# Two passes of 512 and 256 columns for three of 256: both parts of the activations side by side under one weight tile

## The chip, the cores and the metric

The kernel runs on one core of one Trainium2 chip. The metric is the device time of one execution in microseconds. TensorE (PE) multiplies, VectorE (DVE), ScalarE (ACT) and GpSimd (POOL) do the rest, and SyncE (SP) issues most of the transfers.

## The reference

Two networks of two layers each run one behind the other on 256 tokens of 1024 features, batch 1, in float32. The first network (conditioning, neighbourhood attention beside a matrix memory, a delta-rule recurrence, squared-ReLU MLPs) also carries 256 context tokens through its first layer. The second has swiglu stages around two mixers and a memory attention. The parts that the change reaches, cut to the products:

```python
def _swiglu(h, w_gu, w_down):                      # w_gu 1024 x 5632, w_down 2816 x 1024
    gate, up = jnp.split(h @ w_gu, 2, axis=-1)
    return (jax.nn.silu(gate) * up) @ w_down

def squared_relu_mlp(h, w1, w2):                   # w1 1024 x 4096, w2 4096 x 1024
    return jnp.square(jax.nn.relu(h @ w1)) @ w2

# first network, layer 1, after its recurrence
x = x + gt_a * o_l                                 # o_l = (...) @ w_o, 1024 x 1024
x = x + gt_m * squared_relu_mlp(modulate(x, sh_m, sc_m), mlp_w1[1], mlp_w2[1])
# second network
for layer in range(2):
    x = x + 0.5 * _swiglu(_rmsnorm(x, ffn_pre_norm[layer]), ...)
    x = x + (_even_mixer if layer == 0 else _mla_mixer)(_rmsnorm(x, mix_norm[layer]), ...)
    x = x + _memory_cross_attention(_rmsnorm(x, xmem_norm[layer]), ...)
    x = x + 0.5 * _swiglu(_rmsnorm(x, ffn_post_norm[layer]), ...)
```

## The kernel before

Activations lie with features on partitions: `x` is eight tiles of 128 features by 256 tokens. Each operand of a product is split into two float32r parts, a high one (`wh`, `xh`) and a low one (`wl`, `xl`), whose sum is exact. `mm3` then takes three passes: high by high, high by low, low by high. Each pass is one matmul with its own load of the stationary operand, a weight unit of 128 by 128.

Weights come as a `Stream` of units. Its `load` fetches a tile of 2048 columns, 1 MB, from SP's queue into one of two `raw` buffers. Each half of 1024 columns, eight units, is copied to `wh` on ScalarE (L71) and the remainder put into `wl` on VectorE (L72); there are four buffers of each, so splits run up to four halves ahead of the products.

`gemm_a` computes a product with features on partitions: for each feature tile of the result it takes a bank `g` of PSUM and runs `mm3` over the feature tiles of the input, with the stationary weight unit and 256 columns (the tokens) moving; then `evac` evicts the bank. In layer 0's MLP the moving operand has 512 columns, since tokens and context tokens stand side by side (`n_cols`). `gemm_b` has the activations stationary and is not touched.

The users of `gemm_a` with 256 columns all lie in the second half of the program: the recurrence's output product (`rwkv_out`, `wo`, with the first three tiles in two cuts), `mlp` with one stream (`mlp1`, `mlp2`), the four swiglu stages (`ffn`; gate and up run the same loop by hand, a gate and an up tile in one bank), `u`, `q` and `k` of the even mixer, and three output projections (`proj_out`). Units: 64, 256 and 256, 4 x (352 + 176), 96, 192.

A stage begins with a norm. `pre_norm` scales each feature tile (`xg`, VectorE), copies the high part (ScalarE, L167), subtracts for the low part (VectorE, L168), and squares it (ScalarE) for a sum that POOL gathers (L495); two matmuls into `t` (L248) add over the partitions. A swiglu applies 1/rms only at its eviction. The order on each engine is set by a scheduler from the order of the code and the tiles' dependencies; each engine then runs its list in order.

Of the kernel before, what the change touches and what calls it, by code (L numbers as in the profile page):

```python
# [9 lines left out]
F32 = mybir.dt.float32  # L10
# [8 lines left out]
P = 128  # L19
# [10 lines left out]
class Stream:  # L30
    """A weight matrix as a row of [128, nb] units, loaded in tiles of WCOL
    columns and split into two float32r parts whose sum is exact."""
# [11 lines left out]
    def load(self, t):  # L44
        """a tile of the matrix on its way"""
# [34 lines left out]
class KB:  # L80
# [32 lines left out]
    def open_psum(self, **banks):  # L113
        """all of PSUM: banks per pool"""
# [4 lines left out]
    def open_gemm(self, n=4):  # L119
        """the pools of the products with weights"""  # L120
# [21 lines left out]
    def row_in(self, name, n, pool=None):  # L142
        """a row of n numbers, the same in all partitions"""
# [8 lines left out]
    def act_set(self, after, name):  # L152
        """load a named activation table right behind an instruction"""
# [5 lines left out]
    def mm3(self, ps, wh, wl, xh, xl, start, stop):  # L159
        """ps += (wh + wl).T @ (xh + xl) in three float32r passes"""  # L160
# [3 lines left out]
        mm(ps, wl, xh, start=False, stop=stop)  # L164

# [55 lines left out]
    def rstd_tok(self, sums, n, width, scale, eps):  # L221
        """(sums * scale + eps) ** -0.5 on a [128, n] tile"""
# [7 lines left out]
    def sumsq(self, pool, xs, kt):  # L230
        """for each x the sum over its feature tiles of x squared: [128, T], the partitions still to add"""
# [12 lines left out]
    def rstd_from(self, acc, n_feat):  # L244
        """token-major 1/rms [128, 2] from the squares' partial sums"""
# [5 lines left out]
    def bcast_tok(self, rs, pool, col=0, n=2):  # L251
        """rs [128 tokens, n] -> [128, n * 128], the same row in all partitions"""
# [11 lines left out]
class Phase:  # L264
    """pools of one phase: tag -> number of buffers, opened together"""
# [20 lines left out]
def bc(ap, axis, n):  # L286
    """ap with a new axis of n equal entries at free position axis"""
# [2853 lines left out]
```

## Time and profile before

| | us |
|---|---|
| median of 3 runs | 2860.93 |
| lowest, highest | 2856.49, 2864.15 |
| profiled execution, span from the first to the last instruction | 2854.8 |
| PE busy in it | 2654.0 (93%) |
| VectorE busy | 1763.1 (62%) |
| ScalarE busy | 1297.4 (45%) |

For the profiled execution the page gives the span only; what lies around it is not in the page. Busy times are unions, so overlapping products count once. The profile's groups bear the line of the helper that issued an instruction, which is why all products stand under L162 to L164 and are told apart by their tiles' names: `xnh`, `xnl` are a normed input's parts, `hh`, `hl` a swiglu's inner activations or an MLP's input, `dh`, `dl` an MLP's inner activations, `ch`, `cl` the input of an output projection.

### The profile page before, as it was taken

What the parts mean: (1) busy time and instruction counts of PE and PEld (TensorE: products, weight loads), DVE (VectorE), ACT (ScalarE), POOL (GpSimd) and SP (SyncE); (2) the same over time, 40 slices, a digit from 0 to 9 for tenths busy, and PEclk for the clock granted to TensorE, in tenths of its full rate; (3) what the DMA queues carried; (4) which work ended last, traced back from release to release, by engine and by line L of the source; (5) the groups of instructions that cost most, each with busy time, mean ns of one, the idle gap of its engine ahead of it and who ended that gap; (6) DMA issues with size and microseconds to landing.
All of it is one profiled execution on the core that took longest, in us unless ns stands there. A gap on an engine that the chain in (4) does not pass through costs nothing.

```text
span 2854.8 us, 52905 instructions
## 1 busy us (share of the span) xinstructions
PE 2654.0 (93%) x22052; PEld 2362.1 (83%) x22052; DVE 1763.1 (62%) x2885; ACT 1297.4 (45%) x2358; POOL 402.5 (14%) x392
## 2 busy tenths in 40 slices
PE   5999999999968879887899999999999999799999
PEld 3977567888757666765899999998999999798999
DVE  4453564334386966885774665776665665765764
ACT  3344333223245541675553544555444444655443
POOL 1210100000044552342100001011001001311100
PEclk9999989999978889998999999999999999999999
DMA  7244735223223675323455455433455554233554
GB/s 274 89 156 152 260 126 191 103 89 104 83 72 107 226 228 114 81 68 96 139 186 179 170 183 198 163 134 119 167 188 177 178 186 172 96 105 110 177 178 148
DMA packets 108142, 426.29 MB, mean 149 GB/s; under 512 B 14334, under 2 KB 50430, under 8 KB 66046
## 3 DMA queue, kind: packets, MB, share of 16 engines
q1 hardware_dynamic: 107326, 420.76, 43.1%
q8 instruction: 173, 2.83, 0.4%
q10 hardware_dynamic: 576, 2.15, 0.2%
q14 instruction: 67, 0.55, 0.1%
HBM read 397.68 MB, written 24.13 MB: 148 GB/s over the span
## 4 chain that ended last, share of the span: by engine, by line
PE 78%; DVE 13%; ACT 4%; POOL 2%; issue 2%; DMA 1%; SPq 0%; ACTq 0%; DVEq 0%; POOLq 0%
PE g L162 20%; PE g L163 20%; PE g L164 20%; PE pG L162 2%; PE pG L163 2%; PE pG L164 2%; DVE pr L2605 2%; DVE N L2607 2%; PE d L1343 2%; PE pX L2623 1%; DVE wl L72 1%; PE pA L2551 1%; POOL acc L495 1%; DVE we L2558 1%; POOL rs L227 1%
## 5 line engine op out<-in xcount | busy, mean ns | idle before, releaser
L72 DVE TENSOR_TENSOR wl<-raw,wh 128x1024 fp32r<-128x1024 f32 x512 | 626.9, 1225 | 427.7 <-ACT wh L71 425.5
L71 ACT CAST wh<-raw 128x1024 fp32r<-128x1024 f32 x512 | 535.2, 1047 | 638.0 <-PE g L163 546.2
L163 PE MATMUL g<-xnl,wh 128*128 128x256 f32 x1504 | 427.9, 285 | 1.0 <-DVE xnl L168 1.0
L162 PE MATMUL g<-xnh,wh 128*128 128x256 f32 x1504 | 427.4, 285 | 1.3 <-ACT xnh L167 1.3
L164 PE MATMUL g<-xnh,wl 128*128 128x256 f32 x1504 | 427.9, 285 | 0.0
L162 PE MATMUL g<-hh,wh 128*128 128x256 f32 (+1 forms) x1216 | 374.4, 308 | 4.9 <-ACT wh L71 3.4
L164 PE MATMUL g<-hh,wl 128*128 128x256 f32 (+1 forms) x1216 | 373.3, 307 | 0.7 <-DVE wl L72 0.7
L163 PE MATMUL g<-hl,wh 128*128 128x256 f32 (+1 forms) x1216 | 373.9, 308 | 0.0
L162 PEld LDWEIGHTS g<-xnh,wh 128*128 128x128 f32 x1504 | 290.5, 193 | 1.7 <-ACT xnh L167 1.7
L163 PEld LDWEIGHTS g<-xnl,wh 128*128 128x128 f32 x1504 | 290.6, 193 | 1.5 <-DVE xnl L168 1.5
L164 PEld LDWEIGHTS g<-xnh,wl 128*128 128x128 f32 x1504 | 290.7, 193 | 0.0
L162 PEld LDWEIGHTS g<-hh,wh 128*128 128x128 f32 x1216 | 234.6, 193 | 17.5 <-ACT wh L71 4.0
L163 PEld LDWEIGHTS g<-hl,wh 128*128 128x128 f32 x1216 | 234.3, 193 | 14.2 <-DVE hl L1382 2.5
L164 PEld LDWEIGHTS g<-hh,wl 128*128 128x128 f32 x1216 | 234.1, 193 | 12.5 <-issue 1.7
L495 POOL TENSOR_TENSOR acc<-acc,sq 128x256 f32<-128x256 f32 x63 | 65.8, 1045 | 863.5 <-ACT sq L494 381.2
L162 PE MATMUL g<-dh,wh 128*128 128x512 f32 (+1 forms) x512 | 172.0, 336 | 0.0
L163 PE MATMUL g<-dl,wh 128*128 128x512 f32 (+1 forms) x512 | 172.0, 336 | 0.0
L164 PE MATMUL g<-dh,wl 128*128 128x512 f32 (+1 forms) x512 | 172.0, 336 | 0.0
L2623 PE MATMUL pX<-ident 128*128 128x256 f32 (+3 forms) x388 | 106.9, 386 | 32.8 <-DVE N L2607 17.9
L163 PE MATMUL g<-wl,hh 128*128 128x256 f32 x448 | 128.4, 287 | 6.9 <-DVE wl L72 6.9
L162 PE MATMUL g<-wh,hh 128*128 128x256 f32 x448 | 131.2, 293 | 3.3 <-ACT wh L71 3.2
L164 PE MATMUL g<-wh,hl 128*128 128x256 f32 x448 | 127.8, 285 | 0.0
(590 smaller groups left out, 5961.7 us busy)
## 6 DMA issues: line engine op xcount, KB each, us to landing
raw<-in_w_mlp SPq DMA_DIRECT2D x64, 1024.0 KB, 4.8
raw<-in_w_ada SPq DMA_DIRECT2D x48, 1024.0 KB, 6.3
raw<-in_w_pre_gu SPq DMA_DIRECT2D x44, 1024.0 KB, 4.8
raw<-in_w_post_gu SPq DMA_DIRECT2D x44, 1024.0 KB, 4.8
raw<-in_w_pre_down SPq DMA_DIRECT2D x22, 1024.0 KB, 4.8
raw<-in_w_post_down SPq DMA_DIRECT2D x22, 1024.0 KB, 4.8
raw<-in_w_ab SPq DMA_DIRECT2D x14, 1024.0 KB, 4.9
d_bk<-h SPq DMA_DIRECT2D x16, 512.0 KB, 3.0
```

What stands on the lines that cost most here:

```text
L71: nc.scalar.copy(h[:, :w], r)
L72: nc.vector.tensor_tensor(l[:, :w], r, h[:, :w].bitcast(F32), op=ALU.subtract)
L162: mm(ps, wh, xh, start=start, stop=False)
L163: mm(ps, wh, xl, start=False, stop=False)
L164: mm(ps, wl, xh, start=False, stop=stop)
L227: nc.gpsimd.tensor_tensor(rs[:, :n], ms[:, :n], self.mhalf[:, :n], op=ALU.pow)
L495: nc.gpsimd.tensor_tensor(acc, acc, sq, op=ALU.add)
L1343: nc.tensor.matmul(ps[32 * j : 32 * j + 32], self.cpad[:, k0 + j, 30 - 2 * n : 62 - 2 * n], raw[:, j * 512 : (j + 1) * 512], start=n == 0 ...
L2551: nc.tensor.matmul(ps[64:, i], bk[:64, i0 + i], we[0][:64, :W, i0 + i], start=True, stop=True)
L2605: nc.vector.tensor_tensor(pr, bc(N[:, k + 1 :, k], 2, k), bc(N[:, k, :k], 1, m), op=ALU.mult)
L2607: row = nc.vector.tensor_tensor(N[:, k + 1 :, :k], N[:, k + 1 :, :k], pr, op=ALU.add)
L2623: mm = self.nc.tensor.matmul(o, self.ident, bc(self.ident[:, :64], 1, cols // 64), start=True, stop=True)
```

## The change

The two parts of an activation become the two halves of one tile: `x2[:, k]` holds 256 columns of the high part and then 256 of the low one. `mm2` multiplies the high weights with all 512 columns in one pass, into a whole bank, and the low weights with the high half in a second pass, into the bank's first half. The bank's two halves must still be added, so each eviction reads both: `both` copies one half on ScalarE and adds the other on VectorE, and an eviction that adds to `x` does so twice. `gemm_w` is `gemm_a` with `mm2`. Gate and up of a swiglu can no longer share a bank; up goes to a bank of the pool `psa`. In the MLP the ReLU moves from ScalarE's eviction into VectorE's square. The core of the diff:

```diff
+    def mm2(self, ps, wh, wl, x, start, stop):
+        mm = self.nc.tensor.matmul
+        mm(ps, wh, x, start=start, stop=False)
+        mm(ps[:, 0], wl, x[:, 0], start=False, stop=stop)
+
+    def halves(self, ps):
+        return ps.rearrange("p (a t) -> p a t", a=2)
+
+    def both(self, out, ps):
+        self.nc.scalar.copy(out, ps[:, 1])
+        self.nc.vector.tensor_tensor(out, ps[:, 0], out, op=ALU.add)
+
+    def gemm_w(self, st, nt, kt, x, evac, lead=0, cuts=2):
...
+        for n in range(lead, nt):
+            o = self.halves(self.psg.tile([P, 512], F32, name="g"))
+            for k in range(kt):
+                wh, wl = st.next()
+                self.mm2(o, wh, wl, x(k), k == 0, k == kt - 1)
+            evac(n, o)
...
     def pre_norm(self, ph, gain, x=None, tagx="xn"):
...
-        xh = ph.tile(tagx + "h", [P, KT, T], F32R)
-        xl = ph.tile(tagx + "l", [P, KT, T], F32R)
+        self.x2 = ph.tile(tagx + "h", [P, KT, 2, T], F32R)
+        xh, xl = self.x2[:, :, 0], self.x2[:, :, 1]
...
     def ffn(self, which, l):
...
-                ps = self.psg.tile([P, 512], F32, name="g").rearrange("p (z t) -> p z t", z=2)
-                for z in range(2):
+                gu = ph.tile("gu", [P, 2, T])
+                for z, (pool, name) in enumerate(((self.psg, "g"), (self.psa, "a"))):
+                    ps = self.halves(pool.tile([P, 512], F32, name=name))
                     for k in range(KT):
                         wh, wl = st.next()
-                        self.mm3(ps[:, z], wh, wl, xh[:, k], xl[:, k], k == 0, k == KT - 1)
-                gu = ph.tile("gu", [P, 2, T])
-                nc.vector.tensor_tensor(gu, ps, bc(rb, 1, 2), op=ALU.mult)
+                        self.mm2(ps, wh, wl, x2[:, k], k == 0, k == KT - 1)
+                    self.both(gu[:, z], ps)
+                nc.vector.tensor_tensor(gu, gu, bc(rb, 1, 2), op=ALU.mult)
...
             def evac(n, ps):
-                nc.vector.scalar_tensor_tensor(self.x[:, n], ps, 0.5, self.x[:, n], op0=ALU.mult, op1=ALU.add)
-
-            self.gemm_a(st, KT, FT, lambda k: hh[:, k], lambda k: hl[:, k], evac)
+                for a in range(2):
+                    nc.vector.scalar_tensor_tensor(self.x[:, n], ps[:, a], 0.5, self.x[:, n], op0=ALU.mult, op1=ALU.add)
+
+            self.gemm_w(st, KT, FT, lambda k: h2[:, k], evac)
...
     def mlp(self, l, mods, ns, between=None):
...
-                    nc.scalar.activation(r, ps, AF.Relu)
-                    nc.vector.tensor_tensor(r, r, r, op=ALU.mult)
+                    if ns == 1:
+                        self.both(r, ps)
+                        nc.vector.scalar_tensor_tensor(r, r, 0.0, r, op0=ALU.max, op1=ALU.mult)
```

The other evictions (`proj_out`, `rwkv_out`, `mlp2`, `u`, `q`, `k`) change in the same two ways. The transfers, POOL's list and everything before the recurrence's output product keep their order.

Three places show what moves on the engines. On PE, in a gate and up stage of the first swiglu, before (`g_...` is the bank, the numbers name one buffer):

```order
L162 MATMUL g_15801<-xnh_14538,wh_15832 128x256
L163 MATMUL g_15801<-xnl_14539,wh_15832 128x256
L164 MATMUL g_15801<-xnh_14538,wl_15833 128x256
L162 MATMUL g_15801<-xnh_14538,wh_15832 128x256
L163 MATMUL g_15801<-xnl_14539,wh_15832 128x256
L164 MATMUL g_15801<-xnh_14538,wl_15833 128x256
```

and with the change:

```order
L170 MATMUL g_14955<-xnh_14001,wh_14958 128x512
L171 MATMUL g_14955<-xnh_14001,wl_14959 128x256
L170 MATMUL g_14955<-xnh_14001,wh_14958 128x512
L171 MATMUL g_14955<-xnh_14001,wl_14959 128x256
L170 MATMUL a_14980<-xnh_14001,wh_14981 128x512
L171 MATMUL a_14980<-xnh_14001,wl_14982 128x256
```

Three products of 256 columns for a weight unit became one of 512 and one of 256; up's units go to a bank `a`.

On VectorE in the same stage, before (`wl` is a split of weights, `gu` the multiplication with 1/rms, `gs` the product of the two halves, `hl` the low part of the result):

```order
L72 TENSOR_TENSOR wl_15767<-raw_15736,wh_15766 128x1024
L522 TENSOR_TENSOR gs_15664<-gs_15664,gu_15662 128x256
L168 TENSOR_TENSOR hl_14612<-gs_15664,hh_14611 128x256
L72 TENSOR_TENSOR wl_15805<-raw_15802,wh_15804 128x1024
L519 TENSOR_TENSOR gu_15728<-g_15669,rb_14609 128x512
L72 TENSOR_TENSOR wl_15833<-raw_15802,wh_15832 128x1024
L522 TENSOR_TENSOR gs_15730<-gs_15730,gu_15728 128x256
```

and with the change (L179 is the addition in `both`, L552 the multiplication with 1/rms, L555 the product, L200 the low part):

```order
L179 TENSOR_TENSOR gu_14844<-g_14845,gu_14844 128x256
L72 TENSOR_TENSOR wl_14982<-raw_14956,wh_14981 128x1024
L179 TENSOR_TENSOR gu_14844<-a_14870,gu_14844 128x256
L552 TENSOR_TENSOR gu_14844<-gu_14844,rb_14071 128x512
L72 TENSOR_TENSOR wl_15014<-raw_15011,wh_15013 128x1024
L555 TENSOR_TENSOR gs_14894<-gs_14894,gu_14844 128x256
L179 TENSOR_TENSOR gu_14899<-g_14900,gu_14899 128x256
L200 TENSOR_TENSOR hh_14073<-gs_14894,hh_14073 128x256
L179 TENSOR_TENSOR gu_14899<-a_14925,gu_14899 128x256
```

Two additions per pair of tiles stand between the splits of weights; the multiplication now reads their result.

On VectorE at the end of `mlp2` and the entry of the first swiglu, before (L1880 evicts the last bank, L486 scales, L168 takes the low part):

```order
L1880 SCALAR_TENSOR_TENSOR x_11285<-g_14383,mods1_103,x_11285 128x256
L486 TENSOR_SCALAR xg_14540<-x_11285,k_vecs2_73 128x256
L486 TENSOR_SCALAR xg_14544<-x_11285,k_vecs2_73 128x256
L72 TENSOR_TENSOR wl_14711<-raw_14680,wh_14710 128x1024
L168 TENSOR_TENSOR xnl_14539<-xg_14540,xnh_14538 128x256
L168 TENSOR_TENSOR xnl_14539<-xg_14544,xnh_14538 128x256
```

and with the change (L1931 evicts, L518 scales, L200 takes the low part):

```order
L1931 SCALAR_TENSOR_TENSOR x_11285<-g_13883,mods1_103,x_11285 128x256
L518 TENSOR_SCALAR xg_14002<-x_11285,k_vecs2_73 128x256
L1931 SCALAR_TENSOR_TENSOR x_11285<-g_13883,mods1_103,x_11285 128x256
L518 TENSOR_SCALAR xg_14006<-x_11285,k_vecs2_73 128x256
L200 TENSOR_TENSOR xnh_14001<-xg_14002,xnh_14001 128x256
L72 TENSOR_TENSOR wl_14157<-raw_14131,wh_14156 128x1024
L200 TENSOR_TENSOR xnh_14001<-xg_14006,xnh_14001 128x256
```

A second evicting pass stands behind the first scaling, and a split of weights moved behind the first low part.

## Rows read from the trace of the kernel before

**Rows 1.** the page, the chain that ended last: shares of the span, by engine and by line

```profile
PE 78%; DVE 13%; ACT 4%; POOL 2%; issue 2%; DMA 1%; SPq 0%; ACTq 0%; DVEq 0%; POOLq 0%
PE g L162 20%; PE g L163 20%; PE g L164 20%; PE pG L162 2%; PE pG L163 2%; PE pG L164 2%; DVE pr L2605 2%; DVE N L2607 2%; PE d L1343 2%; PE pX L2623 1%; DVE wl L72 1%; PE pA L2551 1%; POOL acc L495 1%; DVE we L2558 1%; POOL rs L227 1%
```

**Rows 2.** stretches; busy us (with instructions) of PE, PEld, DVE, ACT, POOL; granted clock, DMA, GB/s

```profile
1388.10:1396.80 8.70, 7.83 (x33) 7.24 (x34) 7.05 (x13) 4.93 (x8) 0.00 (x0) 0.50 0.25 75
1485.00:1577.20 92.20, 92.20 (x770) 92.17 (x769) 47.96 (x56) 36.80 (x43) 0.00 (x0) 1.00 0.55 187
1577.20:1589.10 11.90, 8.78 (x52) 7.73 (x51) 10.37 (x21) 6.92 (x18) 6.61 (x8) 0.86 0.31 110
1589.10:1710.80 121.70, 121.70 (x1017) 121.70 (x1016) 82.81 (x106) 59.66 (x87) 0.00 (x0) 1.00 0.53 180
```

**Rows 3.** the timeline of PE in a gate and up stage: start, modelled duration, product

```profile
1649.94 0.28 PE L162 MATMUL g<-xnh,wh 128*128 128x256 f32 x1
...
1651.14 0.28 PE L163 MATMUL g<-xnl,wh 128*128 128x256 f32 x1
```

**Rows 4.** the timeline of PE in layer 0's squared-ReLU MLP

```profile
640.04 0.39 PE L162 MATMUL g<-hh,wh 128*128 128x512 f32 x1
...
641.40 0.39 PE L162 MATMUL g<-hh,wh 128*128 128x512 f32 x1
```

**Rows 5.** groups of products by line and shape: count, busy us, mean ns of one

```profile
L162 PE MATMUL g<-xnh,wh 128*128 128x256 f32 x1504 | 427.4, 285 | 1.3 <-ACT xnh L167 1.3
L162 PE MATMUL g<-hh,wh 128*128 128x256 f32 x960 | 273.5, 285 | 3.4 <-ACT wh L71 3.4
...
L162 PE MATMUL g<-ch,wh 128*128 128x256 f32 x256 | 73.1, 288 | 1.4 <-ACT ch L167 1.4
...
L162 PE MATMUL g<-dh,wh 128*128 128x256 f32 x256 | 72.4, 283 | 0.0
```

**Rows 6.** the timeline of PE where gate products stand among others

```profile
55.23 0.28 PE L164 MATMUL g<-wh,hl 128*128 128x256 f32 x1
55.35 0.40 PE L162 MATMUL a<-hh,wgh 128*100 128x512 f32 x1
55.58 0.40 PE L163 MATMUL a<-hl,wgh 128*100 128x512 f32 x1
55.81 0.28 PE L162 MATMUL g<-wh,hh 128*128 128x256 f32 x1
```

**Rows 7.** the timeline of PE at the entry of `mlp1`, half clock

```profile
1390.94 0.41 PE L162 MATMUL g<-hh,wh 128*128 128x256 f32 x1
...
1393.29 0.41 PE L164 MATMUL g<-hh,wl 128*128 128x256 f32 x1
```

**Rows 8.** groups of VectorE from 1412 to 1853 us, by shape

```profile
L72 DVE TENSOR_TENSOR wl<-raw,wh 128x1024 fp32r<-128x1024 f32 x148 | 181.2, 1224 | 103.1 <-ACT wh L71 103.0
L519 DVE TENSOR_TENSOR gu<-g,rb 128x512 f32<-128x512 f32 x22 | 15.2, 691 | 11.2 <-PE g L164 11.2
...
L168 DVE TENSOR_TENSOR hl<-gs,hh 128x256 fp32r<-128x256 f32 x22 | 9.3, 425 | 9.9 <-ACT hh L167 9.9
L522 DVE TENSOR_TENSOR gs<-gs,gu 128x256 f32<-128x256 f32 x22 | 9.2, 418 | 0.5 <-ACT gs L521 0.5
...
L527 DVE SCALAR_TENSOR_TENSOR x<-g,x 128x256 f32<-128x256 f32 x8 | 3.4, 423 | 4.0 <-PE g L164 4.0
L571 DVE TENSOR_TENSOR qk<-g,rb 128x256 f32<-128x256 f32 x8 | 3.3, 419 | 0.7 <-PE g L164 0.7
```

**Rows 9.** the timeline at the entry of the first swiglu stage

```profile
1577.41 0.48 DVE L1880 SCALAR_TENSOR_TENSOR x<-g,mods,x 128x256 f32<-128x256 f32 x1 [0.69 <-PE g L164]
...
1579.65 6.37 POOL L495 TENSOR_TENSOR acc<-acc,sq 128x256 f32<-128x256 f32 x7 [196.43 <-DVE wl L72]
```

**Rows 10.** the waits of PE from 1400 us on: us in total, times, longest

```profile
PE t L248 <- POOL acc L495: 15.0, 8, 3.6
```

**Rows 11.** the page, DMA issues: count, KB each, us from issue to landing

```profile
raw<-in_w_pre_gu SPq DMA_DIRECT2D x44, 1024.0 KB, 4.8
```

More of the change, by code (lines that the diff above doesn't have):

```diff
@@ L164, in mm3 @@
         mm(ps, wl, xh, start=False, stop=stop)
+    def mm2(self, ps, wh, wl, x, start, stop):
[8 more added lines that the diff above has]
+    def gemm_w(self, st, nt, kt, x, evac, lead=0, cuts=2):
+        ws = [[st.next() for _ in range(kt)] for _ in range(lead)]
+        os = [self.halves(self.psg.tile([P, 512], F32, name="g")) for _ in range(lead)]
+        for ks in (range(c * kt // cuts, (c + 1) * kt // cuts) for c in range(cuts if lead else 0)):
+            for n in range(lead):
+                for k in ks:
+                    self.mm2(os[n], *ws[n][k], x(k), k == 0, k == kt - 1)
+        for n in range(lead):
+            evac(n, os[n])
+        for n in range(lead, nt):
[4 more added lines that the diff above has]
+            evac(n, o)
     def split(self, h, l, src, eng=None):
@@ L522, in ffn, with proj_out @@
                 nc.vector.tensor_tensor(gs, gs, gu[:, 1], op=ALU.mult)
-                self.split(hh[:, n], hl[:, n], gs)
+                self.split(h2[:, n, 0], h2[:, n, 1], gs)
             st = Stream(self, self.i[f"w_{which}_down{l}"], KT * FT, P)
             def evac(n, ps):
-                nc.vector.scalar_tensor_tensor(self.x[:, n], ps, 0.5, self.x[:, n], op0=ALU.mult, op1=ALU.add)
-            self.gemm_a(st, KT, FT, lambda k: hh[:, k], lambda k: hl[:, k], evac)
-    def proj_out(self, name, ch, cl):
+                for a in range(2):
+                    nc.vector.scalar_tensor_tensor(self.x[:, n], ps[:, a], 0.5, self.x[:, n], op0=ALU.mult, op1=ALU.add)
+            self.gemm_w(st, KT, FT, lambda k: h2[:, k], evac)
+    def proj_out(self, name, c2):
         nc = self.nc
         def evac(n, ps):
-            nc.vector.tensor_tensor(self.x[:, n], ps, self.x[:, n], op=ALU.add)
-        self.gemm_a(Stream(self, self.i[name], KT * KT, P), KT, KT, lambda k: ch[:, k], lambda k: cl[:, k], evac)
+            for a in range(2):
+                nc.vector.tensor_tensor(self.x[:, n], ps[:, a], self.x[:, n], op=ALU.add)
+        self.gemm_w(Stream(self, self.i[name], KT * KT, P), KT, KT, lambda k: c2[:, k], evac)
     def even_mixer(self, filler=None):
         nc = self.nc
-        with self.phase("ev", xnh=1, xnl=1, xg=2, acc=1, sq=2, rb=1, qk=1, v=1, u=1, g=1, cat=1, c1=1, sb=4, sb2=4, gw=4) as ph:
+        with self.phase("ev", xnh=1, xg=2, acc=1, sq=2, rb=1, qk=1, v=1, u=1, g=1, cat=1, c1=1, sb=4, sb2=4, gw=4) as ph:
             xh, xl, acc = self.pre_norm(ph, self.vec("mix_norm", 0))
@@ L707, in mem_kv @@
         nc = self.nc
-        with self.phase(f"kv{l}", xnh=1, xnl=1, xg=2, acc=1, sq=2, xj=1, xq=2, mem=1) as ph:
+        with self.phase(f"kv{l}", xnh=1, xg=2, acc=1, sq=2, xj=1, xq=2, mem=1) as ph:
             mem = ph.tile("mem", [P, KT, T])
@@ L2856, in rw_pools @@
         ph.__enter__()
-        self.ch, self.cl = (ph.tile("c", [P, KT, T], F32R, name=n) for n in ("ch", "cl"))
+        self.c2 = ph.tile("c", [P, KT, 2, T], F32R, name="ch")
+        self.ch, self.cl = self.c2[:, :, 0], self.c2[:, :, 1]
         yield "set", "pools"
@@ L2917, in evac @@
         def evac(n, ps):
-            nc.vector.scalar_tensor_tensor(self.x[:, n], ps, self.mod(mods, 2, n, 0), self.x[:, n], op0=ALU.mult, op1=ALU.add)
-        self.gemm_a(self.wo, KT, KT, lambda k: self.ch[:, k], lambda k: self.cl[:, k], evac, lead=3)
+            for a in range(2):
+                nc.vector.scalar_tensor_tensor(self.x[:, n], ps[:, a], self.mod(mods, 2, n, 0), self.x[:, n], op0=ALU.mult, op1=ALU.add)
+        self.gemm_w(self.wo, KT, KT, lambda k: self.c2[:, k], evac, lead=3)
         self.ro.__exit__(None, None, None)
```

71 lines of the change are left out of this document (43 added, 28 removed).

## The prediction

> **What bounds the kernel now.** I read the chain that ended last first. It lies on TensorE for 78% of the span, and three lines of one helper, the three passes of `mm3` into tile `g`, hold 20% each [rows 1]. So most of the span is matmuls in a row. The stretches of the last half show which kind of bound that is [rows 2]. From 1485.0 to 1577.2 us PE is busy for 92.20 of 92.20 us while VectorE is busy for 47.96; from 1589.1 to 1710.8 us PE is busy all the time, VectorE for 82.81 of 121.70 and ScalarE for 59.66. Nothing there waits for weights or for an eviction. Only at the entry of a stage does PE starve: from 1577.2 to 1589.1 us it is busy for 8.78 of 11.90 us, VectorE for 10.37.
>
> PE's busy time does not say what a product costs, since products overlap. I take the distance from start to start in the timeline. At the granted clock 1.00, which is 2.4 GHz, ten products of 256 columns lie between 1649.94 and 1651.14 us: 120.0 ns each [rows 3]. Six products of 512 columns lie between 640.04 and 641.40 us: 226.7 ns each [rows 4]. The 256 columns more cost 106.7 ns, so a product of 256 columns is 106.7 ns for its columns and 13.3 ns that come once per product, whatever its width.
>
> **What the change removes.** A weight unit now takes two products, one of 512 and one of 256 columns, where it took three of 256: 226.7 + 120.0 = 346.7 ns for 360.0. The columns stay at 768; one fixed part of 13.3 ns goes. The units that change are counted by the groups of their first pass: 1504 (gate and up of the four swiglu stages, 1408, and u, q, k of the even mixer, 96), 960 (four down projections, 704, and `mlp1`, 256), 256 (`mlp2` with 256 columns) and 256 (three output projections and the recurrence's) [rows 5]. Together 2976 units; 2976 x 13.3 ns = 39.6 us.
>
> No row shows the new rhythm, 512 and 256 in turn. The nearest are the gate products early on, woven among others [rows 6]: 256 columns before 512 take 0.12 us, 512 before 256 take 0.23 us. Those 512-column products have a stationary tile of 100 columns, and they take 0.23 us among themselves too. I take the sum of the two pure rhythms, 346.7 ns. The bounds are 320.0 ns (768 columns and no fixed part, a gain of 119 us) and 360.0 ns (nothing gained).
>
> At half clock there is nothing to gain: with the granted clock at 0.50 (1.2 GHz), eleven products from 1390.94 to 1393.29 us take 214 ns each, which is their columns alone at that clock [rows 7]. In the 8.7 us of that stretch 33 products run [rows 2], 11 units, 0.1 us of gain that doesn't come.
>
> The Trainium skill, page "TensorE: Matmul & The Clock Gate", section "Back-to-back issue gap", puts the warm gap at N / 2.4 + 2.5 ns and so the fixed part at 2.5 ns. The trace disagrees: 13.3 ns here. By the page the gain would be 2976 x 2.5 ns = 7.4 us, by the rows 39.6 us. I go by the rows.
>
> **What it adds, and what hides it.** Each eviction grows. In gate and up, a pair of tiles gets two ScalarE copies and two VectorE additions. A VectorE pass over 256 columns with one operand in PSUM takes 0.42 us [rows 8]. A pair of tiles then costs VectorE two splits of weights (2 x 1.22), two additions (0.84), the multiplication with 1/rms (0.69), the product (0.42) and the split's low part (0.43): 4.82 us, where it cost 3.98. PE needs 16 x 346.7 ns = 5.55 us for the pair. So VectorE goes from 69% to 87% and stays under PE. In `mlp1` a tile costs it 1.22 + 0.42 (the addition) + 0.42 (the square with its maximum) + 0.43 = 2.49 us beside PE's 2.77, 90%: the tightest place. ScalarE has half its time free [rows 2]; even at 0.42 us a copy, 44 copies more add 18.5 us to its 59.66. The order of VectorE's rows shows that the additions stand between splits of weights that are made up to four tiles ahead, and that evictions have three banks of each kind, so a late addition is not felt until it is some 8 us late (three tiles of 2.77 us). I cost the evictions inside a stage at nothing; without that cover they would cost 0.42 us per tile.
>
> Weights come in tiles of 1 MB, 4.8 us from issue to landing [rows 11], and PE will use one up in 5.55 us instead of 5.76. Tight, but two such tiles are held at a time and four halves of one stand split ahead of PE, so I cost it at nothing; if a tile came late, its lateness would show as PE waiting for ScalarE's `wh`.
>
> At the end of a stage the eviction is on the path: the next stage's norm needs the last feature tile. There a second VectorE pass stands, 0.42 us in the seven stages that add plainly or with a half [rows 8], 0.48 us in the two with a modulation [rows 9]. The last swiglu ends at the output's transfer. 7 x 0.42 + 2 x 0.48 = 3.9 us lost.
>
> At the entry of a stage the first product reads both parts at once, so it waits for the low part too, and the order shows VectorE's fourth split of weights standing among the first low parts. Against that, PE waits there anyway for the sum of squares: POOL's seven additions take 6.37 us [rows 9], and PE lost 15.0 us in eight waits for them [rows 10]. The bounds are nothing and one split of weights, 1.22 us, for each of the seven entries (six norms and the recurrence's output). I take 0.4 us, nearer to nothing because that other wait ends last: 2.8 us lost.
>
> **The sum.** 39.6 - 0.1 - 3.9 - 2.8 = 32.8 us off the span of 2854.8 us, 2822.0 us. The page gives the profiled execution its span alone; the three runs have a median of 2860.93 us, 6.1 us above that span. So 2828.1 us, 1.1% less. The three runs lie within 0.3% of one another, and a difference of under 0.3% (8.6 us) is what I call no change.
>
> **The rivals.**
> *The fixed part isn't saved* (no change). It could come with each 256 columns that share a weight tile's turn, so that the pair 512 + 256 still takes 360 ns. For it: no row shows the pair in steady rhythm. Against it: 226.7 ns, not 240, for 512 [rows 4]. Then only the losses are left: 2860.9 + 6.8 = 2867.7 us, 0.2% more. The Trainium skill's 2.5 ns, on the page named above, would land beside it: 2860.9 - 7.4 + 6.8 = 2860.3 us. The trace speaks against that with 13.3 ns.
>
> *VectorE becomes the bound* (no change). If each of its additions also waits out its ScalarE copy, some 0.5 us apiece (an estimate: 0.42 us for a pass over 256 columns [rows 8] and a little for the hand-over), a gate-and-up pair takes 4.82 + 1.0 = 5.82 us and a tile of `mlp1` 2.99 us. 88 pairs lose 0.06 us each against 5.76, 32 tiles 0.11 us against 2.88: 8.8 us lost; the other 1312 units still gain 17.5 us; the ends and entries take 6.7. Net 2.0 us gained: 2858.9 us. It decides from 5.55 us a pair on. Against it: VectorE has splits of later tiles to do in the meantime.
>
> *The clock falls at stage ends* (slower). At the entry of `mlp1` PE ran its first 8.7 us of products at 0.50 [rows 2]. The gaps at the ends grow, and a fall could follow at the other eight too; a stretch at 0.50 costs half its length. With 13 us at each end that is 8 x 6.5 = 52 us: 2828.1 + 52 = 2880 us. It decides from 10.4 us at each end on (8 x 5.2 = 41.6 us, which is 2869.7 us). For it: the clock did fall here, and reads 0.86 at the next entry [rows 2]. Against it: the gaps grow by under 1 us, and between 1589 and 1711 us it is back at 1.00.
>
> *More is saved.* If the load of the next weights is what makes the fixed part, it could vanish behind the 512 columns and leave one in three products: 333.3 ns a unit, 79.4 - 6.8 us, 2788 us. Against it: 512 columns on 512 keep their 13.3 ns [rows 4].
>
> **How the numbers follow.** The forecast has 0.77 (its own range is 2816 to 2842 us, from the entries' and ends' bounds and a fixed part between 10 and 16 ns), the unsaved fixed part 0.07, VectorE as the bound 0.06, the clock 0.05, the larger gain 0.05. Faster by over 0.3%: 0.77 + 0.05 and 0.01 of the VectorE case, 0.83; same 0.13; slower 0.04. The range takes in the forecast's own and reaches a little towards both neighbours: 2808 to 2846 us.
>
> **What would show it.** In the down projections and `mlp2`: starts at 227 and 120 ns in turn, and stages shorter by 3.7%, such as 88.8 us for the 92.2 of [rows 2]. In gate and up: PE busy throughout, VectorE near 87%. At the ends two evicting passes in a row and the wait for the sum of squares half a microsecond later. PE waiting for `wl` or an addition inside a stage, a unit at 360 ns, or new stretches at 0.50 would show me wrong.

## The result, and the profile after

The changed kernel takes 2830.56 us, the median of 4 runs (2824.86 to 2833.30), where the kernel before took 2861.08 us (4 runs, 2856.49 to 2864.15). The ratio is 0.9894, with a 95% interval from 0.9877 to 0.9910: 30.5 us less, for 2828.1 us forecast. A second group of four runs gave 2826.96 us and a ratio of 0.9885 (0.9871 to 0.9898).

The page of the changed kernel: the span, the busy time of the engines, and the chain that ended last by engine and by line.

```profile
span 2829.6 us, 47460 instructions
...
PE 2629.2 (93%) x19076; PEld 2200.4 (78%) x19076; DVE 1854.1 (66%) x3177; ACT 1353.4 (48%) x2546; POOL 407.0 (14%) x392
...
PE 76%; DVE 14%; ACT 4%; POOL 3%; issue 2%; DMA 1%; SPq 0%; ACTq 0%; POOLq 0%; DVEq 0%
PE g L170 17%; PE g L171 9%; PE g L162 8%; PE g L164 8%; PE g L163 8%; PE a L170 6%; PE a L171 3%; PE pG L162 2%; PE pG L163 2%; PE pG L164 2%; DVE N L2660 2%; DVE pr L2658 2%; PE d L1382 2%; PE pX L2676 1%; DVE wl L72 1%
```

TensorE still holds the chain, 76% for the 78% of [rows 1], and its busy share is 93% in both. The three passes of `mm3` into `g` no longer lead; the two of `mm2` do. The answer to [rows 5], the groups of the wide product by shape:

```profile
L170 PE MATMUL g<-xnh,wh 128*128 128x512 f32 x800 | 287.3, 399 | 3.4 <-DVE xnh L200 3.4
L170 PE MATMUL a<-xnh,wh 128*128 128x512 f32 x704 | 252.7, 398 | 0.0
L170 PE MATMUL g<-hh,wh 128*128 128x512 f32 x704 | 246.6, 396 | 0.0
...
L170 PE MATMUL g<-ch,wh 128*128 128x512 f32 x256 | 91.8, 402 | 3.1 <-DVE ch L200 2.8
L170 PE MATMUL g<-x,wh 128*128 128x512 f32 x256 | 91.7, 401 | 3.4 <-ACT wh L71 3.4
...
L170 PE MATMUL g<-d,wh 128*128 128x512 f32 x256 | 88.8, 391 | 0.0
```

800 + 704 + 704 + 256 + 256 + 256 = 2976 wide products (gate's and up's halves now stand in `g` and `a`), the count of the prediction. The stretches that answer to [rows 2], and two more of the second half; the columns are the same (busy us of PE, PEld, VectorE, ScalarE, POOL; granted clock; DMA):

```profile
1487.10:1575.80 88.70, 88.70 (x514) 78.13 (x512) 52.09 (x66) 37.07 (x43) 0.00 (x0) 1.00 0.55 190
1575.80:1589.30 13.50, 10.22 (x40) 7.95 (x39) 9.48 (x22) 6.60 (x17) 7.38 (x8) 0.75 0.29 106
1589.30:1706.10 116.80, 116.80 (x676) 102.14 (x675) 94.50 (x147) 71.99 (x129) 0.00 (x0) 1.00 0.54 186
1706.20:1767.10 60.90, 60.90 (x353) 53.30 (x352) 42.61 (x57) 28.87 (x40) 6.76 (x6) 1.00 0.55 190
2120.60:2182.80 62.20, 62.20 (x354) 53.91 (x353) 42.25 (x55) 28.46 (x39) 6.74 (x6) 1.00 0.56 191
```

`mlp2` takes 88.70 us where it took 92.20: 256 units of 346.5 ns. The forecast was 88.8 us. PE is busy throughout, there as in gate and up (116.80 of 116.80 us). VectorE is at 81% there, for 87% forecast. But the last two rows are the down projections of pre0 and post0, 176 units each: 60.90 us make 346.0 ns a unit, 62.20 us make 353.4 ns. The timeline of PE in `mlp2` and in that slower stage:

```profile
1519.68 0.39 PE L170 MATMUL g<-d,wh 128*128 128x512 f32 x1
1519.91 0.28 PE L171 MATMUL g<-d,wl 128*128 128x256 f32 x1
...
1521.06 0.39 PE L170 MATMUL g<-d,wh 128*128 128x512 f32 x1
```

```profile
2149.95 0.40 PE L170 MATMUL g<-hh,wh 128*128 128x512 f32 x1
...
2150.32 0.40 PE L170 MATMUL g<-hh,wh 128*128 128x512 f32 x1
...
2150.66 0.40 PE L170 MATMUL g<-hh,wh 128*128 128x512 f32 x1
...
2151.01 0.40 PE L170 MATMUL g<-hh,wh 128*128 128x512 f32 x1
...
2151.38 0.40 PE L170 MATMUL g<-hh,wh 128*128 128x512 f32 x1
```

In the first, four units start within 1.38 us, one like the other. In the second, starts of wide products lie 0.37, 0.34 and 0.35 us apart and then 0.37 again: every third unit is 10 ns longer, and the mean is 353.3 ns. The granted clock is 1.00 in both, and nothing is waited for.

For a ledger I took from PE's timelines the time between the last weight product of one stage and the last of the next; the units and their rhythm are in the last column. "Again" is the second trace of either kernel.

| stretch up to the last product of | before | before, again | after | after, again | units: ns each after / again |
|---|---|---|---|---|---|
| the recurrence (first product of its output projection) | 1356.7 | 1354.5 | 1362.5 | 1354.1 | none changed |
| its output projection | 23.0 | 23.0 | 22.6 | 22.6 | 64: 353.3 / 353.3 |
| `mlp1` | 105.2 | 105.0 | 101.9 | 103.5 | 256: 346.7 / 353.3 |
| `mlp2` | 92.2 | 92.2 | 88.7 | 90.5 | 256: 346.7 / 353.3 |
| pre0 | 196.9 | 196.9 | 191.4 | 191.4 | 528: 346.7 / 346.7 |
| even mixer and its projection | 157.1 | 157.1 | 155.9 | 156.1 | 160: about 353 in both |
| cross attention and its projection | 69.8 | 69.9 | 71.2 | 71.2 | 64: about 353 in both |
| post0 | 196.4 | 196.4 | 188.5 | 188.5 | 528: 353.3 / 353.3 |
| pre1 | 192.5 | 192.5 | 189.0 | 185.6 | 528: 353.3 / 346.7 |
| MLA mixer, cross attention, projection | 261.9 | 264.1 | 266.4 | 266.6 | 64: 346.7 / 353.3, read from its last 32 |
| post1 | 197.3 | 197.8 | 185.4 | 185.1 | 528: 346.7 / 346.7 |
| to the end of the span | 5.6 | 5.6 | 6.1 | 6.1 | none |

The first traces close as follows. Products: 1632 units gained 13.3 ns and 1344 gained 6.7 ns, 30.7 us. What is left of each stage when units times rhythm is taken off (360 ns before) changed by +1.5 us in pre0, +1.8 in the cross attention, -4.4 in post0, -4.9 in post1, +0.5 at the end, and by 0.2 or less elsewhere: 5.5 us gained. Together 36.2 us. Two stretches in which the change leaves the instructions as they were took more time in this one execution, 5.8 us up to the recurrence's projection and 5.3 us around the MLA mixer; 36.2 - 5.8 - 5.3 = 25.1 us, beside 2854.8 - 2829.6 = 25.2 us, the difference of the spans.

post0 and post1 gained where nothing was forecast to be gained: at their entries. The waits of PE that answer to [rows 10], from 1400 us on:

```profile
PE t L280 <- POOL acc L527: 8.5, 7, 2.7
```

8.5 us for the 15.0 of [rows 10].

### The profile page after: what moved, and what is told of

Read it like the earlier page. It is cut to its first block, busy times and chain, and to the rows that moved or that the text cites. A ratio compares the mean times of both kernels' runs of the same rounds, so it can differ in the third digit from the quotient of the medians.

```text
span 2829.6 us, 47460 instructions
## 1 busy us (share of the span) xinstructions
PE 2629.2 (93%) x19076; PEld 2200.4 (78%) x19076; DVE 1854.1 (66%) x3177; ACT 1353.4 (48%) x2546; POOL 407.0 (14%) x392
## 4 chain that ended last, share of the span: by engine, by line
PE 76%; DVE 14%; ACT 4%; POOL 3%; issue 2%; DMA 1%; SPq 0%; ACTq 0%; POOLq 0%; DVEq 0%
PE g L170 17%; PE g L171 9%; PE g L162 8%; PE g L164 8%; PE g L163 8%; PE a L170 6%; PE a L171 3%; PE pG L162 2%; PE pG L163 2%; PE pG L164 2%; DVE N L2660 2%; DVE pr L2658 2%; PE d L1382 2%; PE pX L2676 1%; DVE wl L72 1%
## 5 line engine op out<-in xcount | busy, mean ns | idle before, releaser
L170 PE MATMUL g<-xnh,wh 128*128 128x512 f32 x800 | 287.3, 399 | 3.4 <-DVE xnh L200 3.4
L170 PE MATMUL a<-xnh,wh 128*128 128x512 f32 x704 | 252.7, 398 | 0.0
L170 PE MATMUL g<-hh,wh 128*128 128x512 f32 x704 | 246.6, 396 | 0.0
L171 PE MATMUL g<-xnh,wl 128*128 128x256 f32 x800 | 224.1, 280 | 0.0
L171 PE MATMUL a<-xnh,wl 128*128 128x256 f32 x704 | 197.3, 280 | 0.0
L171 PE MATMUL g<-hh,wl 128*128 128x256 f32 x704 | 196.4, 279 | 0.0
L170 PEld LDWEIGHTS g<-xnh,wh 128*128 128x128 f32 x800 | 150.8, 188 | 40.9 <-DVE xnh L200 2.7
L170 PEld LDWEIGHTS a<-xnh,wh 128*128 128x128 f32 x704 | 132.9, 189 | 31.9
L171 PEld LDWEIGHTS g<-xnh,wl 128*128 128x128 f32 x800 | 151.3, 189 | 0.1
L171 PEld LDWEIGHTS a<-xnh,wl 128*128 128x128 f32 x704 | 133.4, 190 | 0.1
L162 PE MATMUL g<-hh,wh 128*128 128x512 f32 x256 | 100.8, 394 | 1.5 <-ACT hh L1420 1.5
```

Of the source, the lines that this page charges most:

```text
L162: mm(ps, wh, xh, start=start, stop=False)
L170: mm(ps, wh, x, start=start, stop=False)
L171: mm(ps[:, 0], wl, x[:, 0], start=False, stop=stop)
```

## The experiments

**The same two kernels once more** (no edit). Of the changed one:

> The changed kernel once more, unedited, for a second trace of it. In its first trace a weight unit (a product of 512 columns and one of 256) takes 346.7 ns in mlp1, mlp2, pre0 and post1, as predicted, but 353.3 ns in the recurrence's output projection, the even mixer, the cross projection, post0 and pre1. If the slower rhythm belongs to the place in the program (its tiles, its banks, what the other engines do there), the same stages show 353.3 ns again. If it comes with the single execution (how a stage's first products happen to start), other stages show it, and the sum over the 2976 units moves by up to 2976 x 6.7 ns = 20 us from one execution to the next. The time: 2830 us within 0.2% either way. The stretches that the change doesn't touch, ahead of 1362 us and between 2375 and 2615 us, move by some us with the clock falls.

Measured: 2826.96 us (4 runs, 2823.01 to 2830.71). The stretch of `mlp2` in this trace, and the first gate and up stretch of pre1:

```profile
1480.20:1570.60 90.40, 90.40 (x513) 78.42 (x513) 52.21 (x67) 36.91 (x43) 0.00 (x0) 1.00 0.56 186
2183.80:2300.70 116.90, 116.90 (x676) 102.23 (x676) 93.49 (x145) 69.81 (x126) 0.00 (x0) 1.00 0.55 184
```

`mlp2` is slow now, 90.40 us for its 256 units (353.1 ns), and pre1, slow before, is at 346.7 ns. So the place alone does not set the rhythm: a stage can take up the one or the other in two executions and then keeps it to its end, with `mlp1` and `mlp2` always alike. Some places did not vary, though: in five traces of kernels with this order of products pre0 always showed 346.7 ns and the even mixer's products 353. What decides it I did not settle. A fall of the clock ahead of the stage does not alone, since `mlp1` begins with a half-clock stretch in every trace and showed 346.7 ns three times and 353.3 ns twice in those five.

> The kernel before once more, unedited, for a second trace. If three narrow products have one rhythm, every steady stage shows 360.0 ns a unit, as in its first trace, and none a second rhythm as the wide ones do. The stretches that the change leaves alone (up to the recurrence's output projection, and the MLA mixer) began and ended 5.8 us later and took 4.7 us longer in the changed kernel's first trace; if those differences are the execution's, through where the clock falls, this trace differs from the first one by some us there as well, and the time is 2860 us within 0.2%.

Measured: 2859.24 us (11 runs), ratio to the other runs of the same kernel 1.0002 (0.9992 to 1.0012). Three narrow products have one rhythm: every steady stage of this trace shows 360 ns, as `mlp2` here (256 units in 92.2 us).

```profile
1481.90:1574.10 92.20, 92.20 (x771) 92.20 (x770) 48.36 (x58) 36.86 (x43) 0.00 (x0) 1.00 0.53 186
```

The ledger's columns of before agree to 0.5 us in every stage that the change touches, and differ by 2.2 us in each of the two stretches that hold other work, up to the recurrence's projection and around the MLA mixer.

**Narrow products, all else as changed.**

```diff
     def mm2(self, ps, wh, wl, x, start, stop):
         mm = self.nc.tensor.matmul
-        mm(ps, wh, x, start=start, stop=False)
+        for a in (slice(0, 2),) if start else (0, 1):
+            mm(ps[:, a], wh, x[:, a], start=start, stop=False)
         mm(ps[:, 0], wl, x[:, 0], start=False, stop=stop)
```

> The wide product is taken apart again: for every k but a tile's first, the high weights take the two halves of x in two products of 256 columns into the two halves of the bank, so 2684 of the 2976 units have three products, and tiles, evictions and additions stay those of the changed kernel. If the gain is one fixed part of 13.3 ns per product, these units take 360.0 ns; against 346.7 ns in 1632 units and 353.3 ns in 1344 of the first trace (nine tenths of either become narrow), 1469 x 13.3 + 1210 x 6.7 ns = 27.6 us come back: 2858 us. If the gain came from the evictions, or from another order of VectorE's work at the stages' ends, the time stays at 2830 us, within 3 us.

Measured: 2855.64 us (12 runs), ratio to before 0.9981 (0.9971 to 0.9992). Against the changed kernel's 2826.96 us, which ran beside it, 28.7 us came back. `mlp2` in it:

```profile
1486.00:1578.00 92.00, 92.00 (x762) 91.64 (x761) 52.25 (x67) 36.89 (x43) 0.00 (x0) 1.00 0.52 183
```

In `mlp2` 32 units are now 95 products. From the last product of `mlp1` to its own last the stage takes 92.1 us, 359.7 ns for each of its 256 units (31 units of 360.0 and one of 346.7 would be 359.6). The gain is in the products. Of the 4.8 us that stay below before, the 292 units that are still wide would make 3.9 us at 13.3 ns. The times alone would not show this, since stages' entries moved too (in this trace the cross attention keeps 52.7 us beyond its products, for 48.6 in the changed kernel); the rhythm does. What the fixed part is paid for stays open: every product here, wide or narrow, has a load of its weights of its own (762 and 761 in that row), so product and load are not told apart.

**Wide beside wide, narrow beside narrow.**

```diff
-    def mm2(self, ps, wh, wl, x, start, stop):
-        mm = self.nc.tensor.matmul
-        mm(ps, wh, x, start=start, stop=False)
-        mm(ps[:, 0], wl, x[:, 0], start=False, stop=stop)
+    def mm2(self, ps, wh, wl, x, start, stop, odd=0):
+        ms = [(ps, wh, x), (ps[:, 0], wl, x[:, 0])]
+        for j, m in enumerate(reversed(ms) if odd else ms):
+            self.nc.tensor.matmul(*m, start=start and j == 0, stop=stop and j == 1)
...
-                self.mm2(o, wh, wl, x(k), k == 0, k == kt - 1)
+                self.mm2(o, wh, wl, x(k), k == 0, k == kt - 1, k % 2)
```

> The two products of every second unit change places, so that PE's products run 512, 256, 256, 512, 512, 256 and so on: a wide one follows a wide one, a narrow one a narrow one, half the time. Columns and count of products are unchanged. If a wide product's 226.7 ns and a narrow one's 120.0 ns hold whatever stands next, and the slow rhythm of 353.3 ns comes from taking turns, two units take 693.3 ns everywhere and the 1344 slow units give back 6.7 ns each, 9 us: 2822 us. If the rhythm is set by something else, some stages are slow here as well and the time stays within 0.2% of 2830 us.

Measured: 2822.80 us (4 runs, 2820.82 to 2825.47), ratio 0.9871 (0.9858 to 0.9884). `mlp2` in this trace:

```profile
1481.80:1571.00 89.20, 89.20 (x515) 77.83 (x513) 51.78 (x65) 36.73 (x42) 0.00 (x0) 1.00 0.56 191
```

256 units in 89.2 us, 348.4 ns, and 348 ns in every other steady stage: one rhythm, between the two, and not the pure sum that was expected. The median lies 4.2 us below that of the changed kernel beside it, 2826.96 us; the intervals of the two ratios overlap (0.9871 to 0.9898 there), so this difference is not clear of the noise, and the rhythm is read from the trace. In that kernel's second trace 1392 units were slow and would give back 5.0 ns each, 1584 were fast and would lose 1.6: 4.4 us. The 9 us of the expectation were counted without that loss and from the first group's median.

**Eight wide, then eight narrow.**

```diff
-    def mm2(self, ps, wh, wl, x, start, stop):
...
+    def run8(self, ps, ws, x, ks, kt):
+        mm = self.nc.tensor.matmul
+        for k, w in zip(ks, ws):
+            mm(ps, w[0], x(k), start=k == 0, stop=False)
+        for k, w in zip(ks, ws):
+            mm(ps[:, 0], w[1], x(k)[:, 0], start=False, stop=k == kt - 1)
...
```

> Eight wide products in a row, with the high parts of eight units, then the eight narrow ones with their low parts (in the down projections eight, eight and six). If taking turns is what makes the two rhythms of the changed kernel and the 348.3 ns of the order 512, 256, 256, 512, then runs of one width show their pure rhythms, 8 x 226.7 + 8 x 120.0 = 2773 ns for eight units, 346.7 ns each in every stage and every execution: 2976 x 1.6 = 4.8 us less than that order's 2822.8 us, 2818 us. If each change of width costs nothing by itself and the 348.3 ns was the order's own, the same. If the slow rhythm comes from something else, stages at 353.3 ns show up and the time is 2823 us or more.

Measured: 2826.41 us (6 runs, 2821.97 to 2838.15), ratio 0.9887 (0.9868 to 0.9905). The expectation fell. The timeline of PE in a gate and up stage:

```profile
2249.90 2.00 PE L169 MATMUL g<-xnh,wh 128*128 128x512 f32 x8
2251.74 1.11 PE L171 MATMUL g<-xnh,wl 128*128 128x256 f32 x8
2252.70 0.86 PE L169 MATMUL a<-xnh,wh 128*128 128x512 f32 x3
```

Eight wide products take 1.84 us from the first to the first narrow one, 230 ns each on average and not 226.7; eight narrow ones take 0.96 us, 120 ns each. That is 350 ns a unit, and 349 to 350 in every steady stage. So there is one rhythm here as well. The single starts tell more. Over the 36 such runs between 2200 and 2300 us, the five wide products that come first behind narrow ones take 233, 236, 228, 232 and 231 ns on average, and the last three 226.7 ns, the price that I took from [rows 4]. The first narrow one behind wide ones takes 113 ns, the others 119 to 120. So it is the turn from narrow to wide that costs, some 27 ns over five products, of which the turn back returns some 7.

**The copy on VectorE.**

```diff
     def both(self, out, ps):
-        self.nc.scalar.copy(out, ps[:, 1])
+        self.nc.vector.tensor_copy(out, ps[:, 1])
         self.nc.vector.tensor_tensor(out, ps[:, 0], out, op=ALU.add)
```

> The copy of a bank's second half moves from ScalarE to VectorE, 0.42 us more on VectorE for each tile that is evicted through the addition. By the prediction's count a pair of gate and up tiles then costs VectorE 4.82 + 0.84 = 5.66 us, over PE's 5.55 us at 346.7 ns a unit and as long as its 5.65 us at 353.3 ns; a tile of mlp1 costs 2.91 us beside PE's 2.77. If VectorE's count decides as the prediction reckoned, the two fast gate and up stages lose 44 x 0.11 = 4.8 us, the two slow ones nothing, mlp1 32 x 0.14 = 4.5 us: 2839 us. If VectorE has other time lost between its rows (its idle time in the first trace is not all waits for work), it is well over, 2850 us and more. If it has room left, the time stays within 3 us of 2830 us.

Measured: 2826.40 us (4 runs, 2822.30 to 2831.92), ratio 0.9884 (0.9870 to 0.9898), no loss. The gate and up stage of pre0 in it:

```profile
1595.00:1695.00 100.00, 100.00 (x579) 88.19 (x578) 94.20 (x168) 50.17 (x74) 0.00 (x0) 1.00 0.58 198
```

VectorE is busy for 94.20 of 100 us and PE still for all of it, at 346.7 ns a unit. By the prediction's count VectorE would need 5.66 us for a pair, 102% of PE's 5.55. The count added each row's duration, and so added, the groups of VectorE in these 100 us do make 105.0 us; the timeline of VectorE in the changed kernel shows why that is too much:

```profile
1649.21 1.23 DVE L72 TENSOR_TENSOR wl<-raw,wh 128x1024 fp32r<-128x1024 f32 x1 [0.48 <-ACT wh L71]
1650.35 0.42 DVE L555 TENSOR_TENSOR gs<-gs,gu 128x256 f32<-128x256 f32 x1
1650.69 0.42 DVE L179 TENSOR_TENSOR gu<-g,gu 128x256 f32<-128x256 f32 x1
```

Where a row waits for nothing, it starts before the row ahead is over: 0.34 us behind a start of 0.42 us (1650.35 to 1650.69), 1.14 us behind one of 1.23 us (1649.21 to 1650.35). The Trainium skill, page "VectorE: DVE Perf Modes", tells of this in the section "Two Vector instructions with no wait between them": a held instruction starts only when all earlier ones have finished. The rows agree in that none of these was held back so, 0.34 us behind a row of 0.42.

**The old output projections.**

```diff
         def evac(n, ps):
-            for a in range(2):
-                nc.vector.tensor_tensor(self.x[:, n], ps[:, a], self.x[:, n], op=ALU.add)
+            nc.vector.tensor_tensor(self.x[:, n], ps, self.x[:, n], op=ALU.add)
-        self.gemm_w(Stream(self, self.i[name], KT * KT, P), KT, KT, lambda k: c2[:, k], evac)
+        self.gemm_a(Stream(self, self.i[name], KT * KT, P), KT, KT, lambda k: c2[:, k, 0], lambda k: c2[:, k, 1], evac)
```

> The changed kernel with only the three output projections (192 of the 2976 units) put back to three products of 256 columns and one evicting pass. That gives VectorE its old order at the entries of post0 and post1: a split of weights stands between the last two evictions into x again, where the changed kernel has none. In the first trace of the changed kernel PE waits 0.8 us for the sum of squares at these two entries, before it waited 3.9 us. If that order is what the change won there, the waits are near 3.9 us again, and 2 x 3.1 + 192 x 13.3 ns (or 6.7) - 3 x 0.4 us (the evicting passes) come back: 6 to 8 us more than the changed kernel, 2834 us. If the shorter waits came from somewhere else (the clock, the faster products before), they stay short and the time stays within 3 us of the changed kernel's 2827 to 2831 us.

Measured: 2828.02 us (4 runs, 2827.50 to 2834.59), ratio 0.9895 (0.9881 to 0.9909). By the expectation's marks the median speaks for its second case, within 3 us of the changed kernel, and not for 2834 us. But it does not tell the two cases apart: a stage's rhythm alone moves it by 3.5 us, and the trace is that of the slowest of the four, 2834.59 us. The waits do, and the trace shows them. The entry of post0 in it, then in the changed kernel: the last two evicting passes into `x`, what stands between them on VectorE, and PE's product that needs the sum of squares, with its wait in brackets.

```profile
1991.21 0.41 DVE L570 TENSOR_TENSOR x<-g,x 128x256 f32<-128x256 f32 x1
...
1991.55 1.21 DVE L72 TENSOR_TENSOR wl<-raw,wh 128x1024 fp32r<-128x1024 f32 x1
...
1992.68 0.82 DVE L518 TENSOR_SCALAR xg<-x,k_vecs 128x256 f32<-128x256 f32 x1
...
1993.42 0.41 DVE L570 TENSOR_TENSOR x<-g,x 128x256 f32<-128x256 f32 x1
...
1996.78 1.01 PE L280 MATMUL t<-ones,acc 128*128 128x1 f32 x4 [3.55 <-POOL acc L527]
```

```profile
1994.73 0.41 DVE L570 TENSOR_TENSOR x<-g,x 128x256 f32<-128x256 f32 x1
...
1995.06 0.63 DVE L200 TENSOR_TENSOR xnh<-xg,xnh 128x256 fp32r<-128x256 f32 x1
...
1995.61 0.41 DVE L570 TENSOR_TENSOR x<-g,x 128x256 f32<-128x256 f32 x1
...
1997.52 0.61 PE L280 MATMUL t<-ones,acc 128*128 128x1 f32 x4 [0.50 <-POOL acc L527]
```

With the old projection a split of weights (1.21 us, from 1991.55) and a multiplication with the next norm's gain stand between the last two evictions, 2.21 us apart; PE waits 3.55 us. In the changed kernel the last two evictions, both of the last tile, stand 0.88 us apart with only a low part between them, and PE waits 0.50 us. Counted from the end of the projection's last product (1991.23 and 1994.47 us), the last eviction starts 2.19 us later in the one and 1.14 us in the other. Both traces of either kernel agree: the waits at the entries of post0 and post1 are 3.6 us in all four cases before and 0.5 us in all four cases after (the expectation read them as 3.9 and 0.8). The clock follows; first this run, then the changed kernel at the entries of post0 and post1:

```profile
1992.80:2001.10 8.30, 4.75 (x20) 4.04 (x18) 4.53 (x10) 3.01 (x5) 2.63 (x3) 0.71 0.66 241
```

```profile
1994.20:2001.80 7.60, 7.10 (x41) 5.75 (x40) 7.00 (x15) 3.53 (x7) 3.61 (x3) 1.00 0.50 154
2638.10:2646.10 8.00, 7.31 (x43) 5.80 (x41) 7.38 (x15) 3.80 (x8) 3.96 (x3) 1.00 0.43 138
```

The granted clock is 0.71 with the long wait and 1.00 with the short one. In the kernel before, it is below 1.00 over the entries of both stages:

```profile
2001.00:2010.00 9.00, 5.37 (x38) 5.16 (x37) 6.27 (x12) 3.42 (x6) 3.16 (x3) 0.88 0.65 224
2651.80:2661.70 9.90, 6.26 (x38) 6.05 (x37) 6.33 (x13) 3.43 (x6) 3.15 (x3) 0.73 0.57 213
```

All the waits of PE for this sum, from 1400 us on, are 13.5 us here and 8.5 us in the changed kernel. post0 and post1 take 190.7 and 190.9 us at 346.7 ns a unit, 7.7 and 7.8 us beyond their products; in the changed kernel that rest is 1.9 and 2.4 us, and 6.3 and 7.2 us in the kernel before. So the order of VectorE's rows is what shortened these entries; its worth is read from traces alone, and no group of runs shows it in the time. One thing may take part of it back: in the five traces with the order 512, 256, post0 ran at 346.7 ns in the two where the clock fell at its entry (0.71 here, 0.74 in the run with one evicting pass) and at 353.3 ns in the three where it did not, which is 3.5 us for its 528 units. Whether the one brings the other is not shown.

**One evicting pass into x.**

```diff
-            for a in range(2):
+            for a in range(1):
                 nc.vector.tensor_tensor(self.x[:, n], ps[:, a], self.x[:, n], op=ALU.add)
```

(and the same in the evictions of the down projections, `mlp2` and the recurrence's projection)

> The changed kernel with one evicting pass into x instead of two, in the recurrence's output projection, mlp2, the four down projections and the three output projections; it leaves out the product of the low part of the activations there. This prices the second pass at the stages' ends. If it is on the path as the prediction reckoned, 0.42 to 0.48 us at each of nine ends go, 3.9 us: 2824 us beside 2827 to 2831 us, and each entry's trace is shorter by that. If VectorE's new order at the ends hides it (the trace of the changed kernel shows the sum of squares at pre1 no later than before), only the last end, behind which nothing stands, gets 0.4 us shorter, and the time stays within 2 us. The two entries behind the cross projections could even lose, if a split of weights stands there between the last evictions again.

Measured: 2825.22 us (6 runs, 2822.28 to 2834.81), ratio 0.9887 (0.9869 to 0.9904), no gain that can be told from the changed kernel. In its trace pre1 takes 189.0 us at 353.3 ns a unit, as in the changed kernel's first one, and the end behind the last product 5.6 us for 6.1. The waits for the sum of squares went up:

```profile
PE t L280 <- POOL acc L527: 14.0, 8, 3.1
```

With one pass the split of weights stands between the last evictions again at the entries of post0 and post1: beyond their products these stages keep 7.0 and 5.9 us, for 1.9 and 2.4 in the changed kernel. Elsewhere something came back, 1.4 us at pre0 and 1.2 us at the cross attention, so the absent gain in time is a sum of both signs. At pre1's entry the second pass is hidden by ScalarE. This is that entry in the changed kernel:

```profile
2182.95 1.05 ACT L71 CAST wh<-raw 128x1024 fp32r<-128x1024 f32 x1 [1.78 <-PE g L170]
2183.01 0.88 DVE L561 SCALAR_TENSOR_TENSOR x<-g,x 128x256 f32<-128x256 f32 x2 [0.59 <-PE g L171]
...
2183.99 0.42 ACT L526 ACTIVATE sq<-x 128x256 f32<-128x256 f32 x1
...
2184.55 1.29 POOL L527 TENSOR_TENSOR acc<-acc,sq 128x256 f32<-128x256 f32 x1 [4.34 <-ACT sq L526]
```

Both passes (one row, x2) are over at 2183.89 us, but ScalarE is at a cast of weights until 2184.00 and starts the square of that tile at 2183.99.

**The best of these.** The alternating order, with the even mixer's output projection alone put back (its edit is the one above under the condition that the weights are the even mixer's).

> The order 512, 256, 256, 512 of the earlier run, with the even mixer's output projection (64 units) put back to three narrow products and one evicting pass. In that run PE waited 3.9 us for the sum of squares behind this projection, where the kernel before waited 1.5 us. If VectorE's evicting passes are late there, the wait is 1.5 us again and 2.4 us are won, less 64 x 11.7 ns = 0.7 us for the products: 2821 us beside 2823 us. It is also a second trace of that order: if its rhythm of 348.3 ns a unit is its own, every steady stage shows it again; if it was one execution's, some show 346.7 or 353.3 ns. A rival: the wait comes from elsewhere and stays, 2823.5 us.

Measured: 2816.93 us (5 runs, 2812.40 to 2822.62), ratio to before 0.9858 (0.9840 to 0.9876), the lowest median here, though its interval overlaps that of the alternating order alone. The wait behind the even mixer's projection, without the edit (3.6 us, for the 3.9 of the expectation) and with it:

```profile
PE t L280 <- POOL acc L527: 3.6, 1, 3.6
```

```profile
PE t L280 <- POOL acc L527: 1.2, 1, 1.2
```

The cross stretch of the ledger took 73.8 us without the edit and 69.7 with it. The steady stages show 348 ns again, `mlp2` 89.0 us, so this rhythm has now stood in two executions. Part of the rest of the gain is this trace's MLA stretch (259.3 us), which no edit touched.

## Why the prediction was right

**The fixed part** was right in kind. It is paid per product and not per 256 columns: with three narrow products in place of two, 28.7 us came back where the step asked for 27.6. **Its size** was right only where a stage runs at 346.7 ns. The step "I take the sum of the two pure rhythms" left out that wide and narrow in turn have two rhythms; about half the units ran at 353.3 ns, and the term of 39.6 us measured 30.7 us. The rival of an unsaved fixed part (360 ns) and that of a larger gain (333.3 ns) are out: no steady stage showed either. So is the 2.5 ns of the Trainium skill's page "TensorE: Matmul & The Clock Gate", section "Back-to-back issue gap", which gives it for a product on its own: by it, as an estimate, the narrow products would have cost 2684 x 2.5 ns = 6.7 us.

**The evictions inside a stage** cost nothing, as forecast, and with more room than forecast: VectorE stayed hidden even with one pass more per tile. The rival with VectorE as the bound is out; the prediction's 4.82 us per pair was too high because it added durations that overlap.

**The ends** (3.9 us) were mis-sized: the trace shows 0.5 us at the last one, and none at the entry of pre1, where ScalarE's cast of weights covers the second pass. At the other stages the traces do not part the end from the entry behind it.

**The entries** (2.8 us) had the wrong sign. pre0 lost 1.5 us and the cross attention 1.8, where end and entry together were forecast at 0.9 and 0.8, but post0 and post1 gained 4.4 and 4.9 us. The wait for the sum of squares, forecast half a microsecond later, came out both ways: behind the even mixer's projection it rose from 1.2 to 2.3 us, most of what the cross attention lost, and at post0 and post1 it fell. The step that failed is that the prediction looked at how long the added passes take and not at which row of VectorE stands between the last two evictions. The second pass moved a split of weights from there, the wait fell from 3.6 us, the longest of [rows 10], to 0.5, and the clock stayed at 1.00 over both entries, where it had read 0.88 and 0.73. So the clock rival went the other way there. At pre0 it came true in small: the clock reads 0.75 over 13.5 us, for 0.86 over 11.9 us in [rows 2]. That is 3.4 us of full clock lost for 1.7, as an estimate from these rows, and so about the 1.5 us that pre0 lost. In the last run above, with both evicting passes there, it reads 0.87 over 13.5 us, and pre0 keeps 7.1 us beyond its products, for 8.4 in the changed kernel and 6.8 before.

The forecast of 32.8 us less thus met medians of 30.5 and 33.5 us in part by luck, because two errors nearly cancelled: 8.8 us too much for the products, 12.2 us too little for ends and entries (6.7 lost forecast, 5.5 gained measured). The 3.4 us between are less than the 8.4 us by which the unchanged stretch up to the recurrence's projection differs between the two traces of the changed kernel. The 6.1 us that the prediction put between span and median were not a constant either. The time of a run lies some 1.8 us above its own span (2831.41 and 2829.6 us in the changed kernel's profiled execution); so the profiled execution of the kernel before took some 2856.6 us, the lowest of the runs shown, and the rest of the 6.1 was that.

## What to carry to other kernels

Price a stream of products by its distances from start to start, and make products wide where a fixed part comes with each; but look for the rhythm of the mix itself, since two pure rhythms need not add up. Price VectorE's rows by their starts as well, or the bound seems nearer than it is. At a stage's end, look at the order of the rows around the last eviction before their durations: at two entries one split of weights ahead of it went with 3 us of waiting and a fall of the clock, more than the second passes that were added there.

## What the hardware showed that was not expected

The same order of 512 and 256 columns ran at 346.7 or at 353.3 ns a unit at the granted clock 1.00, steady over a whole stage, and the same stage showed the one or the other in two executions of the same kernel. Three narrow products (360.0 ns), the order 512, 256, 256, 512 (348.3 ns) and runs of eight (349.4 ns) each had one rhythm in the traces taken. What sets it stays open. In the runs of eight a wide product took 226.7 ns only from the sixth on; the first five behind narrow ones took 228 to 236 ns. The clock of an entry went with a wait of a few microseconds: 0.71 with one of 3.55 us, 1.00 over the same entry with one of 0.50 us.
